# Delta-rule heads of a two-layer diffusion backbone: the two head pairs computed in step instead of one after the other

## The chip, the cores and the metric

One core of a Trainium2 chip runs the whole program in one launch. The metric is the device time of that core in microseconds (us), median of several executions.

## The reference, cut to what matters

Two layers over 256 context and 256 latent tokens. Each layer projects the normed tokens (`w_in`), feeds three groups of heads (A: softmax attention, B: HGRN2 recurrence, C: gated DeltaNet), projects their outputs (`w_out`), and ends with a gated MLP with a short convolution. The change is in group C: four heads of width 64, both directions, chunks of 64 tokens. For one head and one chunk, in short form:

```
kk    = einsum('bhtd,bhsd->bhts', k, k)
tri   = eye(c) + where(strict, beta * kk * decay, 0)
sol   = triangular_solve(tri, [v * beta, k * beta * exp(gc)])     # u, w
v_new = u - w @ state
out   = (q * exp(gc)) @ state + ((q k^T) * decay) @ v_new
state = exp(g_last) * state + (k * exp(g_last - gc))^T @ v_new
```

## The kernel before, in words

Activations lie transposed, 128 channels on the partitions and 512 tokens along a row, columns 0 to 255 context and 256 to 511 latent. A dense product (`dense`, `dense_gen`, L276 to L296) takes a weight block split into a rounded high part and a rest (`wload`: a DMA on SP's queue, a cast on ScalarE, a subtraction on VectorE or GpSimd) and issues three matmuls for each 128 channels, L292 to L294 in the projections of the heads.

Group C has four heads in two pairs. A pair lies on the 128 partitions, one head on partitions 0 to 63 (its lower half), the other on 64 to 127. `gdn` (L594 to L754) works on one pair and is run for pair 0, then for pair 1 (`gd` in `mixers`, L1132). Inside, it runs over the context half and the latent half of the tokens, four chunks each, both directions at once:

- a prologue (L621 to L650): decay matrices `E1`, `X`; the cumulative decay `gb` by a matmul with the block matrix `bones`; token-major copies of k and v (`relay`); the product `kk`;
- the inverse of `tri` by doubling (L663 to L690). Five levels each have a product `rt`, a masking on VectorE (L679), a product `dT`, and a subtraction on VectorE (L689) into `MT`; beside them a copy on ScalarE (L684) and a transpose on VectorE (L685) feed `dT`;
- a scan over four chunks (L708 to L736): `ks` = k times state, two VectorE operations (L716), `vn` = the solved rows, a copy on ScalarE (L720), `kv` = k times the new values, two VectorE operations (L734) for the next state;
- the output products `go` (L749).

Each of these is a set of 64x64 matmuls. A matmul whose operands lie on one half and whose result lies on one half uses one quarter of the 128x128 array, a corner. `bmm` (L518) issues them for both heads of the pair: rows 0 to 63 to columns 0 to 63, and rows 64 to 127 to columns 64 to 127, so two of the four corners. Both write one PSUM bank, each its own half. Group B's products (`hs` L847, `hu`, `ho`) use all four corners, its `hs` with one bank for each half of the rows. The trace counts two matmul instructions for each such fp32 matmul, so a row of the order with x8 is x16 in the trace.

What sets the order: `weave` (L1025) takes steps from several generators in turn, in the shares of the table `RATE` (in-projections, group C, group B, attention, modulation; the sixth number is group C's share while only projections run beside it); the framework's scheduler then fixes each engine's order. TensorE executes its matmuls in that order, so one that has to wait holds up all behind it. Group C's pages have the tag `g` (5 pages, 4 taken by a pair and half); 512-column temporaries share `r2` (16).

Of the kernel before, what the change touches and what calls it, by code (L numbers as in the profile page):

```python
# [20 lines left out]
P = 128  # L21
# [13 lines left out]
R2, RAW, WHI, WLO = 16, 4, 3, 2  # L35
# [9 lines left out]
RATE = ((103, 220, 32, 136, 15, 12), (69, 192, 60, 63, 5, 9))  # L45
# [35 lines left out]
for _name, _w in (("ident", 128), ("ones", 128), ("sel", 2), ("sel8", 16), ("eps", 1), ("one", 1), ("bones", 128),  # L81
                  ("perm", 128), ("i64", 64), ("inc2", 128), ("ninc2", 128), ("pstr2", 128), 
# [7 lines left out]
def constants():  # L90
# [10 lines left out]
    put("bones", same)  # L101
    pm = np.zeros((P, P))
# [41 lines left out]
class Kernel:  # L144
    def __init__(self, ctx, tc, I, out, dbg=None):
# [6 lines left out]
        self.BUFS = {"h": 8, "g": 5, "fk": 2, "qk": 5, "kq": 2, "r2": R2, "d2": 3, "g2": 3, "h2": 5, "hv": 2, "vt": 2, "hq": 1, "ht": 1, "raw": RAW, "whi": WHI, "wlo": WLO}  # L152
        self.uid = 0
        self.ring = itertools.cycle(["g"] * 5 + ["kq"] * 2 + ["fk"] * 4)
# [369 lines left out]
    def relay(self, p, dst, srcs):  # L524
# [69 lines left out]
    def gdn(self, ly, hp, G, kq, v, last, res):  # L594
        nc = self.nc
        k, q = kq[:, 0, :], kq[:, 1, :]
        o = None
        ck = lambda t: t.rearrange("p (c t) -> p c t", t=64)
        hgm = self.C("hgm").rearrange("p (l t) -> p l t", t=64)
        for t, scale, l in ((k, 1.0, 0), (q, 0.125, NCTX if last else 0)):  # L600
            sq = self.tmp("g2", "l2")
            nc.scalar.activation(sq[:, l:], t[:, l:], AF.Square)
            ps = self.bank("g", "l2")
            nc.tensor.matmul(ps[:, l:], self.C("bones"), sq[:, l:], start=True, stop=True)
            self.act(sq[:, l:], ps[:, l:], AF.Ln, bias=self.C("eps"))
            self.act(sq[:, l:], sq[:, l:], AF.Exp, scale=-0.5)
            nc.vector.scalar_tensor_tensor(t[:, l:], t[:, l:], scale, sq[:, l:], ALU.mult, ALU.mult)
        yield
        carry = None
        for hf in range(2):  # L610
            out = hf == 1 or not last
            sel = lambda n: G[n][:, 16 * hp + 8 * hf:16 * hp + 8 * hf + 8]
            b64 = lambda n: sel(n).unsqueeze(2).to_broadcast([P, 8, 64])
# [3 lines left out]
            kc, qc, vc = (ck(t[:, 256 * hf:256 * hf + 256]) for t in (k, q, v))  # L617
            pA, pB = self.pg("g", "gA"), self.pg("g", "gB")
            E1, X = pA[:, 0:512], pA[:, 512:1024]
            eG, tok = pB[:, 0:512], pB[:, 512:1024]  # L620
            nc.vector.tensor_tensor(s4(E1), m4("inc2"), sel("la").rearrange("p (s c) -> p s c", s=2).unsqueeze(3).to_broadcast([P, 2, 4, 64]), ALU.mult)  # L621
            pb = self.bank("g", "gb")
            nc.tensor.matmul(pb, self.C("bones"), E1, start=True, stop=True)
            self.act(eG, pb, AF.Exp)
            nc.vector.tensor_tensor(ck(X), ck(pb), b64("gc"), ALU.subtract)
            yield
            self.relay("g", tok, [(k, 256 * hf, 256 * hf + 256), (v, 256 * hf, 256 * hf + 256)])
            ktok, vtok = ck(tok[:, 0:256]), ck(tok[:, 256:512])
            yield
            if out:  # L630
                for s in range(2):
                    nc.vector.scalar_tensor_tensor(s4(E1)[:, s], s4(X)[:, s], 0.0, m4("ninc2")[:, s], ALU.min, ALU.add)
                self.act(E1, E1, AF.Exp)
            for s in range(2):
                nc.vector.scalar_tensor_tensor(s4(X)[:, s], s4(X)[:, s], 0.0, m4("pstr2")[:, s], ALU.max, ALU.add)
            self.act(X, X, AF.Exp, scale=-1.0)
            nc.gpsimd.tensor_tensor(ck(X), ck(X), b64("beta"), ALU.mult)
            N = X[:, 0:256]
            nc.vector.tensor_tensor(N, X[:, 0:256], X[:, 256:512], ALU.add)
            pk = self.bank("g", "kk")  # L640
            n2 = 2 if out else 1
            pkv = pk.rearrange("p (c s t) -> p c s t", s=2, t=64)
            for c in range(4):
                a = 256 * hf + 64 * c
                for h in (0, 64):
                    nc.tensor.matmul(pkv[h:h + 64, c, 0:n2, :], k[h:h + 64, a:a + 64], kq[h:h + 64, 0:n2, a:a + 64], start=True, stop=True)
            nc.vector.tensor_tensor(ck(N), ck(N), pkv[:, :, 0, :], ALU.mult)
            if out:
                nc.vector.tensor_tensor(s4(E1), s4(E1), two(pkv[:, :, 1, :]), ALU.mult)
            yield  # L650
            gl = self.small("gl", 8, 4)
            ap = eG[:, 0:1]
# [4 lines left out]
            qe, SC = ck(eG), ck(E1)
            pC = self.pg("g", "gC")
            MT, Mx, mtx = pC[:, 0:512], pC[:, 512:768], pC[:, 768:1024]
            nc.scalar.copy(ck(MT), self.C("i64").unsqueeze(1).to_broadcast([P, 8, 64]))  # L660
            Nv, MTv = ck(N), ck(MT)
            for lev in range(LEVELS):
                b = 1 << lev  # L663

                def joint(c0, c1, bit0):
                    ap = MT[:, 256 * bit0 + 64 * c0:256 * bit0 + 64 * c0 + 1]
# [4 lines left out]
                rt = self.tmp("g2", "rt")[:, 0:256]  # L671
                if lev:
                    ps = self.bank("g", "rt")
                    self.bmm(ck(ps), lambda c: Nv[:, c, :], lambda c: joint(c, c + 1, 0), range(4))
                    src = ps[:, 0:256]
                else:
                    src = mtx
                    nc.vector.transpose(mtx, N)
                nc.vector.tensor_tensor(ck(rt), ck(src), hgm[:, lev, :].unsqueeze(1).to_broadcast([P, 4, 64]), ALU.mult)  # L679
                if lev == 0:  # L680
                    nc.vector.tensor_tensor(joint(0, 4, 0), joint(0, 4, 0), nb(rt), ALU.subtract)
# [5 lines left out]
                ps2 = self.bank("g", "dT")  # L687
                self.bmm(ck(ps2), lambda c: ck(Mx)[:, c, :], lambda c: ck(rt)[:, c, :], range(4))
                nc.vector.tensor_tensor(joint(0, 4, 0), joint(0, 4, 0), nb(ps2[:, 0:256]), ALU.subtract)  # L689
                yield  # L690
            pF = self.pg("g", "gF")
            kt, R, U, Sst = pF[:, 0:512], pF[:, 512:1024], X, pC[:, 512:1024]

            def scaled(dst, src, n):
                nc.gpsimd.tensor_tensor(s4(dst), two(src), sel(n).rearrange("p (s c) -> p s c", s=2).unsqueeze(3).to_broadcast([P, 2, 4, 64]), ALU.mult)

            scaled(R, vtok, "beta")
            scaled(kt, ktok, "kd")
            yield
            rv, uv, kv, sv = ck(R), ck(U), ck(kt), ck(Sst)  # L700
# [687 lines left out]
```

## Time and profile before

| | |
|---|---|
| time, median of 3 runs | 1443.58 us (1442.61 to 1451.51) |
| the profiled execution, its own time | 1446.47 us |
| its span, first to last instruction | 1444.7 us |
| TensorE matmuls busy | 1349.8 us, 93% |
| VectorE, ScalarE, GpSimd busy | 898.0, 650.4, 390.5 us |
| chain of work that ended last | PE 74%, DVE 14%, ACT 4%, POOL 3%, DMA 3%, issue 2% |

PE is TensorE, DVE VectorE, ACT ScalarE, POOL GpSimd. The span falls into stages: first projections of layer 0 up to 78 us, its three head groups with the rest of the projections from 78 to 400, the out-projection and MLP to 875, the first projections of layer 1 to 930, its head groups to 1190, the rest to the end. Group C runs in the two head stages alone.

### The profile page before, as it was taken

How to read it: one execution, taken by the hardware profiler on the slowest of the kernel's cores; microseconds unless marked ns; L12 is line 12 of the kernel's file. 1: busy time of each engine (PE TensorE's matmuls, PEld its weight loads, DVE VectorE, ACT ScalarE, POOL GpSimd, SP SyncE). 2: the span in 40 equal slices, each digit the busy share in tenths (PEclk: the TensorE clock that was granted, in tenths of full speed). 3: DMA queues.
4: the chain of work that ended last, by engine and by line, in shares of the span. 5: the costliest groups of instructions: out<-in, count | busy, mean ns of one | idle time of the engine just before them, and what ended most of it. 6: DMA issues, size and time to landing. Idle time of an engine off the chain costs nothing.

```text
span 1444.7 us, 26549 instructions
## 1 busy us (share of the span) xinstructions
PE 1349.8 (93%) x10712; PEld 1073.9 (74%) x10712; DVE 898.0 (62%) x1721; ACT 650.4 (45%) x1169; POOL 390.5 (27%) x370
## 2 busy tenths in 40 slices
PE   5999989999998999999999988999899989899996
PEld 2777656666787678888888887986676647799995
DVE  3573576858557775435544568766887635676765
ACT  4362424534365544324423446663353335565553
POOL 1020032201055222202210365111411005555554
PEclk8999999999899999999999999999999989999998
DMA  8512413222246663333323334532211255465552
GB/s 303 189 59 88 148 43 105 88 88 104 82 134 209 208 208 109 103 94 96 102 90 100 102 121 152 158 125 97 91 59 73 75 201 207 133 187 177 190 173 76
DMA packets 56283, 185.90 MB, mean 129 GB/s; under 512 B 6368, under 2 KB 10464, under 8 KB 56160
## 3 DMA queue, kind: packets, MB, share of 16 engines
q1 hardware_dynamic: 56160, 184.20, 38.6%
q8 instruction: 84, 1.38, 0.4%
q14 instruction: 39, 0.32, 0.1%
HBM read 182.08 MB, written 2.10 MB: 127 GB/s over the span
## 4 chain that ended last, share of the span: by engine, by line
PE 74%; DVE 14%; ACT 4%; POOL 3%; DMA 3%; issue 2%; SPq 0%; DVEq 0%; POOLq 0%; ACTq 0%
PE up L283 8%; PE up L284 8%; PE up L282 8%; PE in L292 6%; PE in L294 5%; PE in L293 5%; PE dn L284 4%; PE dn L283 4%; PE dn L282 4%; PE ada L316 2%; DVE wlo L272 2%; PE sc L993 2%; PE dT L522 1%; DMA raw<-ada_w 1%; PE rt L522 1%
## 5 line engine op out<-in xcount | busy, mean ns | idle before, releaser
L272 DVE TENSOR_TENSOR wlo<-raw,whi 128x1024 fp32r<-128x1024 f32 (+2 forms) x241 | 296.7, 1232 | 271.6 <-issue 93.8
L268 ACT CAST whi<-raw 128x1024 fp32r<-128x1024 f32 (+1 forms) x244 | 249.1, 1023 | 136.0 <-PE dn L284 98.9
L284 PE MATMUL up<-h,whi 128*128 128x256 f32 (+1 forms) x768 | 249.0, 325 | 1.3 <-DVE h L440 0.7
L282 PE MATMUL up<-h,whi 128*128 128x256 f32 (+1 forms) x768 | 248.5, 324 | 1.2 <-ACT h L437 1.1
L283 PE MATMUL up<-h,wlo 128*128 128x256 f32 (+1 forms) x768 | 248.1, 324 | 0.9 <-DVE wlo L272 0.9
L292 PE MATMUL in<-h,whi 128*128 128x512 f32 (+1 forms) x496 | 183.8, 371 | 2.5 <-DVE kq L476 2.2
L272 POOL TENSOR_TENSOR wlo<-raw,whi 128x256 fp32r<-128x256 f32 (+1 forms) x111 | 128.4, 1158 | 194.8 <-ACT whi L268 90.3
L293 PE MATMUL in<-h,wlo 128*128 128x512 f32 (+1 forms) x496 | 176.4, 356 | 1.1 <-DVE wlo L272 0.9
L294 PE MATMUL in<-h,whi 128*128 128x512 f32 (+1 forms) x496 | 177.3, 358 | 0.0
L282 PEld LDWEIGHTS up<-h,whi 128*128 128x128 f32 x768 | 145.9, 190 | 19.4 <-issue 4.2
L284 PEld LDWEIGHTS up<-h,whi 128*128 128x128 f32 x768 | 146.1, 190 | 16.5 <-issue 1.7
L283 PEld LDWEIGHTS up<-h,wlo 128*128 128x128 f32 x768 | 146.0, 190 | 15.7 <-issue 2.5
L283 PE MATMUL dn<-gT,wlo 128*128 128x256 f32 (+1 forms) x400 | 128.4, 322 | 3.4 <-DVE wlo L272 3.4
L282 PE MATMUL dn<-gT,whi 128*128 128x256 f32 (+1 forms) x400 | 128.5, 322 | 2.7 <-ACT gT L299 2.7
L284 PE MATMUL dn<-gT,whi 128*128 128x256 f32 (+1 forms) x400 | 128.2, 321 | 0.7 <-POOL gT L301 0.7
L1220 POOL TENSOR_TENSOR u<-u 128x512 f32<-128x512 f32 (+1 forms) x44 | 44.4, 1009 | 279.4 <-DVE u L476 257.9
L292 PEld LDWEIGHTS in<-h,whi 128*128 128x128 f32 x496 | 95.0, 191 | 21.7 <-issue 6.9
L294 PEld LDWEIGHTS in<-h,whi 128*128 128x128 f32 x496 | 95.1, 192 | 12.9 <-issue 1.5
L293 PEld LDWEIGHTS in<-h,wlo 128*128 128x128 f32 x496 | 95.3, 192 | 11.4 <-DVE wlo L272 1.9
L472 ACT ACTIVATE u<-up,vec 128x256 f32<-128x256 f32 (+1 forms) x96 | 61.8, 644 | 75.2 <-PE up L284 75.2
L283 PEld LDWEIGHTS dn<-gT,wlo 128*128 128x128 f32 x400 | 77.5, 194 | 9.2 <-DVE wlo L272 4.0
L282 PEld LDWEIGHTS dn<-gT,whi 128*128 128x128 f32 x400 | 77.5, 194 | 8.2 <-ACT gT L299 3.1
(278 smaller groups left out, 2414.2 us busy)
## 6 DMA issues: line engine op xcount, KB each, us to landing
raw<-ada_w SPq DMA_DIRECT2D x96, 512.0 KB, 4.3
raw<-w_up SPq DMA_DIRECT2D x96, 512.0 KB, 3.5
raw<-w_in SPq DMA_DIRECT2D x68, 512.0 KB, 3.7
raw<-w_down SPq DMA_DIRECT2D x32, 512.0 KB, 3.5
raw<-w_out SPq DMA_DIRECT2D x24, 512.0 KB, 3.6
raw<-w_down SPq DMA_DIRECT2D x24, 384.0 KB, 3.0
x<-xT SPq DMA_DIRECT2D x16, 256.0 KB, 5.8
x_spill<-x SPq DMA_DIRECT2D x8, 128.0 KB, 2.1
```

What stands on the lines that cost most here:

```text
L268: nc.scalar.copy(hi[:, :cols], raw[:, :cols])
L272: e.tensor_sub(lo[:, a:b], raw[:, a:b], hi[:, a:b].bitcast(F32))
L282: nc.tensor.matmul(ps, wh[:, k, :], ah, start=first and k == ks[0], stop=False)
L283: nc.tensor.matmul(ps, wl[:, k, :], ah, start=False, stop=False)
L284: nc.tensor.matmul(ps, wh[:, k, :], al, start=False, stop=last and k == ks[-1])
L292: nc.tensor.matmul(ps, wh[:, k, :], ah, start=k == 0, stop=False)
L293: nc.tensor.matmul(ps, wl[:, k, :], ah, start=False, stop=False)
L294: nc.tensor.matmul(ps, wh[:, k, :], al, start=False, stop=k == n - 1)
L316: nc.tensor.matmul(ps[32 * g:32 * g + 32, :], self.cs[:, k, :], w[:, kk, :], start=k < 4, stop=k >= 4, tile_position=(0, 32 * g))
L472: nc.scalar.activation(dst, ps, AF.Identity, scale=w3[1], bias=bias)
L522: self.nc.tensor.matmul(pv[h:h + 64, n], l[h:h + 64], r[h:h + 64], start=True, stop=True)
L1220: self.nc.gpsimd.tensor_mul(us[0][:, lo:], us[0][:, lo:], us[1][:, lo:])
```

## The change

`gdn` takes both pairs and does every step for pair 0 and pair 1 together. Pair 1's heads are exchanged: gates, `alog`, `dt` and the token-major copies of its pair stand on the other half, so that its products go from rows 0 to 63 to columns 64 to 127 and from rows 64 to 127 to columns 0 to 63. A new `quad` issues the matmuls of a chunk for both pairs, each pair with a bank of its own. `vn` keeps the same half for rows and columns in both pairs; the part of `go` that reads pair 1's state has become a product `gi` of its own, added by VectorE. New are a matrix `obones` and a matmul `gs` (exp(gc) of pair 1 on exchanged halves), and two half-height copies on ScalarE instead of one full copy for pair 1 at each level.

Pages: `g` 7 instead of 5 (seven taken by a half), `r2` 14 instead of 16, group B's page `ht` gone (its folds go into the page of `F2`), the output of group C is written over q, four of the eight `y` tiles of out-projection and MLP lie in the page `hq`. `RATE` is set anew.

```diff
-R2, RAW, WHI, WLO = 16, 4, 3, 2
+R2, RAW, WHI, WLO = 14, 4, 3, 2
-RATE = ((103, 220, 32, 136, 15, 12), (69, 192, 60, 63, 5, 9))
+RATE = ((121, 197, 32, 218, 37, 8), (53, 64, 15, 50, 5, 7))
-                    ab.append(kind + d * 4 + hp * 2 + h2)
+                    ab.append(kind + d * 4 + hp * 2 + (h2 ^ hp))
-        self.BUFS = {"h": 8, "g": 5, "fk": 2, "qk": 5, "kq": 2, "r2": R2, "d2": 3, "g2": 3, "h2": 5, "hv": 2, "vt": 2, "hq": 1, "ht": 1, "raw": RAW, "whi": WHI, "wlo": WLO}
+        self.BUFS = {"h": 8, "g": 7, "fk": 2, "qk": 5, "kq": 2, "r2": R2, "d2": 3, "g2": 3, "h2": 5, "hv": 2, "vt": 2, "hq": 1, "raw": RAW, "whi": WHI, "wlo": WLO}
+    def new_ys(self):
+        t = self.pg2("hq", "y")
+        return [t[:, 512 * i:512 * i + 512] for i in range(4)] + [self.tmp("r2", "y") for i in range(4)]
+    def quad(self, items):
+        for out, l, r, start, stop in items:
+            self.nc.tensor.matmul(out, l, r, start=start, stop=stop)
-    def gdn(self, ly, hp, G, kq, v, last, res):
+    def gdn(self, ly, G, kq, v, last, res):
+        HP = range(2)
+        H = [slice(0, 64), slice(64, 128)]
...
+                nc.vector.tensor_tensor(ck(X[hp]), ck(pb), b64(hp, "gc"), ALU.subtract)
+                if hp:
+                    pb = self.bank("g", "gs")
+                    nc.tensor.matmul(pb, bones[1], E1[hp], start=True, stop=True)
+                self.act(eG[hp], pb, AF.Exp)
...
-                    ps = self.bank("g", "rt")
-                    self.bmm(ck(ps), lambda c: Nv[:, c, :], lambda c: joint(c, c + 1, 0), range(4))
+                    ps = [self.bank("g", "rt") for hp in HP]
+                    for c in range(4):
+                        self.quad((ck(ps[hp])[H[g ^ hp], c, :], Nv[hp][H[g], c, :], joint(MT[hp][H[g]], c, c + 1, 0), True, True)
+                                  for hp in HP for g in range(2))
...
-                nc.scalar.copy(nb(mtx), joint(0, 4, 1))
-                nc.vector.transpose(Mx, mtx)
+                nc.scalar.copy(nb(mtx[0]), joint(MT[0], 0, 4, 1))
+                for g in range(2):
+                    nc.scalar.copy(nb(mtx[1][H[1 - g]]), joint(MT[1][H[g]], 0, 4, 1))
+                for hp in HP:
+                    nc.vector.transpose(Mx[hp], mtx[hp])
...
+                ps = [self.bank("g", "vn") for hp in HP]
+                for hp in HP:
+                    for s, j in enumerate(js):
+                        self.quad((ck(ps[hp])[H[g], s, :], MTv[hp][H[g], j, :], rv[hp][H[g], j, :], True, True) for g in range(2))
+                    nc.scalar.copy(pair(U[hp], i), ck(ps[hp][:, 0:128]))
...
         def gd():
+            go = {}
+            yield from self.gdn(ly, G, kq, gv, last, go)
             for hp in range(2):
-                go = {}
-                yield from self.gdn(ly, hp, G, kq[hp], gv[hp], last, go)
                 mix[6 + hp] = self.head_end(go[hp], self.V(ly, "gdn"), gg[hp], 1.0 / 64, self.C("bones"), qlo, "g", "r2", "g")
```

How the rows of an engine stand now, at three places. First TensorE in the context half of layer 0, at the first `rt` with a matmul (`in` is a dense product, `gC` holds `MT`, `gA` holds the matrix to invert). Before, pair 0 alone:

```order
L293 MATMUL in_891<-h_131,wlo_888 128x512
L294 MATMUL in_891<-h_131,whi_887 128x512
L522 MATMUL rt_902<-gC_871,gA_741 64x64 x8
L292 MATMUL in_891<-h_132,whi_887 128x512
L293 MATMUL in_891<-h_132,wlo_888 128x512
```

The same place of the changed kernel:

```order
L294 MATMUL in_1081<-h_136,wlo_1078 128x512
L295 MATMUL in_1081<-h_136,whi_1077 128x512
L602 MATMUL rt_1109<-gC_1053,gA_814 64x64 x2
L602 MATMUL rt_1110<-gC_1054,gA_815 64x64 x2
L602 MATMUL rt_1109<-gC_1053,gA_814 64x64 x2
L602 MATMUL rt_1110<-gC_1054,gA_815 64x64 x2
L602 MATMUL rt_1109<-gC_1053,gA_814 64x64 x2
L602 MATMUL rt_1110<-gC_1054,gA_815 64x64 x2
L602 MATMUL rt_1109<-gC_1053,gA_814 64x64 x2
L602 MATMUL rt_1110<-gC_1054,gA_815 64x64 x2
L293 MATMUL in_1141<-h_129,whi_1137 128x512
```

The eight matmuls of pair 1, which stood some hundred rows further down, now alternate with pair 0's two by two, so that four neighbours take four corners. In 28 of the 40 sets of `rt` and `dT` they stand so throughout, in 8 the first few stand pair by pair, in 4 all of one pair stand before the other's.

Second, TensorE in the scan, the same half (`kq` holds k and q, `gF` the right-hand sides). Before, one chunk of pair 0:

```order
L522 MATMUL ks_1344<-gC_871,kq_140 64x64 x4
L292 MATMUL in_1385<-h_129,whi_1381 128x512
L293 MATMUL in_1385<-h_129,wlo_1382 128x512
L294 MATMUL in_1385<-h_129,whi_1381 128x512
L522 MATMUL vn_1351<-gF_1276,gC_871 64x64 x4
L292 MATMUL in_1385<-h_130,whi_1381 128x512
L293 MATMUL in_1385<-h_130,wlo_1382 128x512
L522 MATMUL kv_1364<-gA_741,gF_1276 64x64 x4
```

Of the changed kernel, `vn` and `kv` of a chunk, with a modulation product between:

```order
L602 MATMUL vn_1545<-gF_1521,gC_1053 64x64 x4
L602 MATMUL vn_1546<-gF_1521,gC_1054 64x64 x4
L317 MATMUL ada_1557<-raw_1558,cs 32x512 x2
L317 MATMUL ada_1557<-raw_1562,cs 32x512 x2
L317 MATMUL ada_1557<-raw_1566,cs 32x512 x2
L317 MATMUL ada_1557<-raw_1570,cs 32x512 x2
L602 MATMUL kv_1584<-gA_814,gB_816 64x64 x2
L602 MATMUL kv_1585<-gA_815,gB_817 64x64 x2
L602 MATMUL kv_1584<-gA_814,gB_816 64x64 x2
L602 MATMUL kv_1585<-gA_815,gB_817 64x64 x2
```

`kv` alternates between the pairs, `vn` does not; each set now holds both pairs and has one stretch of other work behind it instead of two.

Third, VectorE between two levels (`wlo` is the split of a weight block). Before:

```order
L689 TENSOR_TENSOR gC_871<-gC_871,dT_947 128x64x2x2
L685 STREAM_TRANSPOSE gC_871<-gC_871 128x256
L272 TENSOR_TENSOR wlo_1033<-raw_1030,whi_1032 128x1024
L679 TENSOR_TENSOR rt_973<-rt_974,consts 128x256
```

Of the changed kernel, a later level:

```order
L721 TENSOR_TENSOR gC_1053<-gC_1053,dT_1293 128x32x2x4
L721 TENSOR_TENSOR gC_1054<-gC_1054,dT_1294 128x32x2x4
L494 COPY raw_1193<-in_1200 128x512
L714 STREAM_TRANSPOSE gC_1053<-gC_1053 128x256
L704 TENSOR_TENSOR rt_1313<-rt_1315,consts 128x256
L704 TENSOR_TENSOR rt_1314<-rt_1316,consts 128x256
L714 STREAM_TRANSPOSE gC_1054<-gC_1054 128x256
```

The VectorE operations of a level are as many as before, but both pairs' stand in one row of work: the next product waits for two of each instead of one.

## Rows read from the trace of the kernel before

**Rows 1.** The two head stages by engine; columns as in its header row.

```profile
core 0: us, PE busy (x) PEld busy (x) DVE busy (x) ACT busy (x) POOL busy (x), PEclk, DMA share, GB/s
78.00:400.00 322.00, 303.89 (x3084) 214.66 (x3084) 209.09 (x508) 134.60 (x291) 49.76 (x42) 0.96 0.26 90
930.00:1190.00 260.00, 247.29 (x2619) 173.05 (x2617) 175.08 (x447) 109.30 (x229) 40.83 (x37) 0.97 0.30 103
```

**Rows 2.** Group C's 64x64 products by line: count, busy us, mean ns, idle before.

```profile
L522 PE MATMUL rt<-gC,gA 64*64 64x64 f32 x640 | 27.8, 226 | 11.9 <-DVE gC L681 8.5 <-DVE ssm L1001 2.2 <-DVE gC L689 0.9
L522 PE MATMUL vn<-gF,gC 64*64 64x64 f32 x256 | 18.8, 242 | 1.3 <-DVE gF L716 1.3
L522 PE MATMUL ks<-gC,kq 64*64 64x64 f32 x224 | 14.1, 238 | 0.3 <-DVE gC L707 0.2
L646 PE MATMUL kk<-kq 64*64 64x128 f32 x96 | 6.5, 275 | 0.0
L749 PE MATMUL go<-gA 64*64 64x64 f32 x192 | 11.6, 221 | 0.0
L749 PE MATMUL go<-gB,gC 64*64 64x64 f32 x176 | 10.7, 218 | 0.0
```

**Rows 3.** Timeline of PE, a set of 16 in dense work: start, us, what.

```profile
114.37 0.39 PE L294 MATMUL in<-h,whi 128*128 128x512 f32 x1
114.69 0.68 PE L522 MATMUL dT<-rt,gC 64*64 64x64 f32 x16
115.30 0.50 PE L292 MATMUL in<-h,whi 128*128 128x512 f32 x1
115.64 0.39 PE L293 MATMUL in<-h,wlo 128*128 128x512 f32 x1
```

**Rows 4.** Timeline of PE, a set of 8.

```profile
159.28 0.40 PE L293 MATMUL in<-h,wlo 128*128 128x512 f32 x1
159.51 0.40 PE L294 MATMUL in<-h,whi 128*128 128x512 f32 x1
159.84 0.45 PE L522 MATMUL ks<-gC,kq 64*64 64x64 f32 x8
160.21 0.50 PE L292 MATMUL in<-h,whi 128*128 128x512 f32 x1
160.55 0.39 PE L293 MATMUL in<-h,wlo 128*128 128x512 f32 x1
```

**Rows 5.** Timeline of PE, group B's 64 in four corners.

```profile
184.68 0.40 PE L294 MATMUL in<-h,whi 128*128 128x512 f32 x1
185.01 1.16 PE L847 MATMUL hs<-raw,kd 64*64 64x64 f32 x64
186.10 0.50 PE L292 MATMUL in<-h,whi 128*128 128x512 f32 x1
186.43 0.39 PE L293 MATMUL in<-h,wlo 128*128 128x512 f32 x1
```

**Rows 6.** Timeline of PE, full-array fp32 products of 128 columns.

```profile
1158.23 1.95 PE L1018 MATMUL do<-wt,vt 128*128 128x128 f32 x16
1160.01 0.60 PE L967 MATMUL vt<-consts,raw 128*128 128x128 f32 x4
```

**Rows 7.** Group C's VectorE operations between products, by line.

```profile
L689 DVE TENSOR_TENSOR gC<-gC,dT 128x256 f32<-128x256 f32 x40 | 16.7, 417 | 23.5 <-PE dT L522 23.5
L685 DVE STREAM_TRANSPOSE gC<-gC 128x256 f32<-128x256 f32 x40 | 17.5, 438 | 8.7 <-ACT gC L684 8.5
L716 DVE SCALAR_TENSOR_TENSOR gF<-ks,sbe,gF 128x64 f32<-128x64 f32 x56 | 13.9, 278 | 14.7 <-PE ks L522 14.5
```

**Rows 8.** Timeline of PE, the first product after a prologue.

```profile
194.10 1.12 PE L522 MATMUL rt<-gC,gA 64*64 64x64 f32 x16 [4.97 <-DVE gC L681]
```

**Rows 9.** Two stretches with the clock at its lower level for a part.

```profile
188.00:201.00 13.00, 8.03 (x81) 5.75 (x80) 8.16 (x14) 2.67 (x5) 4.65 (x3) 0.74 0.12 40
375.00:400.00 25.00, 24.77 (x312) 17.82 (x313) 13.43 (x48) 11.57 (x37) 0.73 (x1) 0.73 0.29 100
```

More of the change, by code (lines that the diff above doesn't have):

```diff
@@ L101, in constants @@
     put("bones", same)
+    put("obones", ~same)
     pm = np.zeros((P, P))
@@ L608, in gdn @@
-        yield
-        carry = None
+        H = [slice(0, 64), slice(64, 128)]
+        for ts, scale, l in ((k, 1.0, 0), (q, 0.125, NCTX if last else 0)):
+            for t in ts:
+                sq = self.tmp("g2", "l2")
+                nc.scalar.activation(sq[:, l:], t[:, l:], AF.Square)
+                ps = self.bank("g", "l2")
+                nc.tensor.matmul(ps[:, l:], self.C("bones"), sq[:, l:], start=True, stop=True)
+                self.act(sq[:, l:], ps[:, l:], AF.Ln, bias=self.C("eps"))
+                self.act(sq[:, l:], sq[:, l:], AF.Exp, scale=-0.5)
+                nc.vector.scalar_tensor_tensor(t[:, l:], t[:, l:], scale, sq[:, l:], ALU.mult, ALU.mult)
+            yield
@@ L634, in gdn @@
[L634 to L640, printed above, removed]
+            kc, qc, vc = ([ck(t[:, 256 * hf:256 * hf + 256]) for t in ts] for ts in (k, q, v))
@@ new lines, in gdn @@
+            yield
+            for hp in HP:
+                self.relay("g", tok[hp], [(t[hp], 256 * hf, 256 * hf + 256) for t in (k, v)], hp)
+                yield
+            ktok, vtok = [ck(t[:, 0:256]) for t in tok], [ck(t[:, 256:512]) for t in tok]
+            for hp in HP:
+                if out:
+                    for s in range(2):
+                        nc.vector.scalar_tensor_tensor(s4(E1[hp])[:, s], s4(X[hp])[:, s], 0.0, m4("ninc2")[:, s], ALU.min, ALU.add)
+                    self.act(E1[hp], E1[hp], AF.Exp)
+                for s in range(2):
+                    nc.vector.scalar_tensor_tensor(s4(X[hp])[:, s], s4(X[hp])[:, s], 0.0, m4("pstr2")[:, s], ALU.max, ALU.add)
+                self.act(X[hp], X[hp], AF.Exp, scale=-1.0)
+                nc.gpsimd.tensor_tensor(ck(X[hp]), ck(X[hp]), b64(hp, "beta"), ALU.mult)
@@ L641, in gdn @@
+            N = [t[:, 0:256] for t in X]
+            pk = [self.bank("g", "kk") for hp in HP]
             n2 = 2 if out else 1
-            pkv = pk.rearrange("p (c s t) -> p c s t", s=2, t=64)
+            pkv = [t.rearrange("p (c s t) -> p c s t", s=2, t=64) for t in pk]
             for c in range(4):
                 a = 256 * hf + 64 * c
-                for h in (0, 64):
-                    nc.tensor.matmul(pkv[h:h + 64, c, 0:n2, :], k[h:h + 64, a:a + 64], kq[h:h + 64, 0:n2, a:a + 64], start=True, stop=True)
@@ L657, in gdn @@
[L657 to L661, printed above, removed]
+                self.quad((pkv[hp][H[h ^ hp], c, 0:n2, :], k[hp][H[h], a:a + 64], kq[hp][H[h], 0:n2, a:a + 64], True, True)
+                          for hp in HP for h in range(2))
+            for hp in HP:
+                nc.vector.tensor_tensor(N[hp], X[hp][:, 0:256], X[hp][:, 256:512], ALU.add)
+                nc.vector.tensor_tensor(ck(N[hp]), ck(N[hp]), pkv[hp][:, :, 0, :], ALU.mult)
+                if out:
+                    nc.vector.tensor_tensor(s4(E1[hp]), s4(E1[hp]), two(pkv[hp][:, :, 1, :]), ALU.mult)
@@ new lines, in gdn @@
+            yield
+            gl = [self.small("gl", 8, 4) for hp in HP]
+            pC = [self.pg("g", "gC") for hp in HP]
+            MT, Mx, mtx = ([t[:, a:b] for t in pC] for a, b in ((0, 512), (512, 768), (768, 1024)))
+            for hp in HP:
+                ap = eG[hp][:, 0:1]
+                nc.gpsimd.tensor_copy(gl[hp].rearrange("p (s c) -> p s c", s=2),
+                                      bass.AP(tensor=ap.tensor, offset=ap.offset, ap=[list(ap.ap[0]), [256 + 63, 2], [64, 4]]))
+                nc.scalar.copy(ck(MT[hp]), self.C("i64").unsqueeze(1).to_broadcast([P, 8, 64]))
@@ new lines, in gdn @@
+                for hp in HP:
+                    nc.vector.transpose(Mx[hp], mtx[hp])
+                yield
+                ps2 = [self.bank("g", "dT") for hp in HP]
+                for c in range(4):
+                    self.quad((ck(ps2[hp])[H[g ^ hp], c, :], ck(Mx[hp])[H[g], c, :], ck(rt[hp])[H[g], c, :], True, True)
+                              for hp in HP for g in range(2))
+                for hp in HP:
+                    nc.vector.tensor_tensor(joint(MT[hp], 0, 4, 0), joint(MT[hp], 0, 4, 0), nb(ps2[hp][:, 0:256]), ALU.subtract)
@@ L690, in gdn @@
                 yield
             pF = self.pg("g", "gF")
[L692 to L698, printed above, removed]
+            R, U, Sst = [pF[:, 512 * hp:512 * hp + 512] for hp in HP], X, [t[:, 512:1024] for t in pC]
@@ L706, in gdn @@
             if carry is not None:
-                nc.vector.tensor_copy(pair(Sst, 0), ck(carry))
+                for hp in HP:
+                    nc.vector.tensor_copy(pair(Sst[hp], 0), ck(carry[hp]))
             for i in range(4):
@@ L1256, in ffn @@
             if ys is None:
-                ys = self.ys = [self.tmp("r2", "yf") for m in range(KT)]
+                ys = self.ys = self.new_ys()
             def down(ss, a, b):
@@ L1310, in run @@
             hT = self.new_pages()
-            self.ys = [self.tmp("r2", "y") for m in range(KT)]
+            self.ys = self.new_ys()
             pending = self.sub_layer(ly, 0, lo, lambda ss, a, b: self.out_proj(ly, mix, ss, a, b), hT)
```

177 lines of the change are left out of this document (84 added, 93 removed).

## The prediction, made before the changed kernel was run

> **What bounds the kernel now.** I read the busy shares by stage first, then the timeline of TensorE (PE) inside the head stages, then what its small products cost there. In the two stages in which group C runs, 322 and 260 us long, PE is busy 303.89 and 247.29 us, so it is idle 18 and 13 us; VectorE (DVE) is busy 209.09 and 175.08 us, about two thirds [rows 1]. PE executes in a fixed order. These stages are therefore as long as the work of PE in them, plus about 31 us in which it waits, plus what a lower clock adds. A cheaper small product moves everything behind it forward, as long as its operands are not late.
>
> **What a set of small products costs.** The dense work around them has a pitch of 0.23 us (159.28 to 159.51) [rows 4]. A set of 16 in two corners moves the second dense matmul behind it from where it would be by 115.64 - 114.37 - 2 x 0.23 = 0.81 us [rows 3]. A set of 8 costs 160.55 - 159.51 - 0.46 = 0.58 us [rows 4]. So eight more cost 0.23 us, 0.029 each, and what is left, 0.81 - 16 x 0.029 = 0.35 us, is paid once for each set: PE runs empty before it and after it. Group B's set of 64 in four corners costs 186.43 - 184.68 - 0.46 = 1.29 us [rows 5]; less 0.35 that is 0.0147 each, half of the pace in two corners. Four corners do run together in this kernel, and the pace of 0.029 is the array's and not that of issuing.
>
> **The change, part by part.**
>
> *The inverse.* `rt` and `dT` (its count is the same) are 640 instructions each, 80 sets of 16 [rows 2]: 80 x 0.81 = 65 us, of which I take off 3 us for sets that stand right beside another small product and share the 0.35. After, 40 sets of 32. By the order 28 alternate throughout, 0.35 + 32 x 0.0147 = 0.82 us; 8 begin pair by pair, I take 1.0; 4 have all of one pair first and cost two sets of 16, 1.62. Together 23 + 8 + 6.5 = 37.5 us. Saved: 24 us.
>
> *The scan.* `ks` and `kv` (same count) are 56 sets of 8 [rows 2], 56 x 0.58 = 32.5 us. After, 28 sets of 16 in four corners at 0.35 + 16 x 0.0147 = 0.585 us, but 8 of them are cut by other work and count as two sets of 8: 20 x 0.585 + 8 x 1.16 = 21 us. Saved: 11.5 us. `vn` is 32 sets of 8 [rows 2], a third of them cut in two by a dense matmul (0.35 more): 18.6 + 3.8 = 22.4 us. After, it stays in two corners and only the sets join: 12 x 0.81 + 4 x 1.16 = 14.4 us. Saved: 8 us.
>
> *Prologue and output.* `kk` has six sets of 16 with 128 columns (0.35 + 16 x 0.058 = 1.28 us) and two with 64 (0.81), 9.3 us [rows 2]; after 3 x 1.28 + 2 x 0.81 = 5.5. Saved: 3.8 us. `go` is 192 + 176 instructions in six sets [rows 2], 368 x 0.029 + 6 x 0.35 = 12.8 us; after, the 192 take four corners (2.8), the 176 stay in two (5.1), with seven switches (2.5): 10.4. Saved: 2.4 us. New is `gs`, four fp32 matmuls of 512 columns. 16 full-array instructions of 128 columns take 1160.01 - 1158.23 = 1.78 us, 0.111 each [rows 6]; 512 columns are 0.445, two instructions 0.89, four times 3.6 us. Added: 3.6 us.
>
> Sum for PE: 24 + 11.5 + 8 + 3.8 + 2.4 - 3.6 = **46 us less**.
>
> *VectorE, ScalarE, GpSimd.* Their operations are as many as before, apart from 20 copies on ScalarE, the adding of `gi` and GpSimd's scaling in two parts. What changes is the wait of one product for the next. Between `rt` and `dT` stand a masking (the same form as L689's 0.417 us) and a transpose (0.438); with both pairs two of each, 0.85 us more. Between `dT` and `rt` a second subtraction, 0.42; around the scan two more operations of 0.278 on either side, 0.56 [rows 7]; from `vn` to `kv` a second copy on ScalarE, taken as 0.28, the size of these. With 20, 20, 14, 14 and 16 such steps that is 17 + 8.4 + 7.8 + 7.8 + 4.5 = 45 us more latency in joined steps. The cover is dense work: by the order most joined sets have 3 to 11 matmuls of 0.23 us, or a modulation or attention product, behind them, and there are half as many sets to cover. I cost it at nothing; with the cover gone it would be those 45 us.
>
> *Prologues.* The worst wait of PE is here: 4.97 us before the first product of pair 0's latent half, on DVE [rows 8]; all of `rt` waits 11.9 us, 8.5 of it there [rows 2]. There were eight prologues, now four with twice the DVE work. Each layer's first is covered by 60 to 90 dense matmuls, the latent ones only by about what one pair had. I take no change, with bounds of 8 us less (these waits gone) and 10 us more (two of 5 us grow to 10).
>
> *Pages, folds, `y` tiles.* At nothing: gates and `y` are read in the MLP, behind whole sets of dense matmuls; the reload of x for the residual is issued behind six of `w_out`'s blocks as before. If the seven pages of `g` make a latent prologue wait for the context half's last reader, its first two DVE operations are late by under 2 us twice.
>
> **A rule that speaks against it.** The pairs of two-corner products write the upper and lower half of one bank. A row of 128 columns takes 0.111 us on the full array [rows 6], so 64 columns take 0.056; these sets run at 0.029, two at a time [rows 3, 4], although both row halves write one bank. The Trainium skill, "TensorEngine Tiling (Array Packing)", section "Gotcha 1: PSUM Pressure", says that different row tiles cannot access the same PSUM bank at once. By that rule the new quads, whose two row halves share each pair's bank, would not overlap as group B's do (its `hs` has a bank for each half). The trace speaks against the rule; it is the first rival.
>
> **The rivals.**
>
> *1. Four corners in this bank layout run no faster than two.* For it: only group B shows four, and with its banks laid out otherwise. Against: the two-corner sets already overlap in one bank [rows 3, 4]. Then only joined sets save: the inverse 61.7 - (36 x 1.28 + 6.5) = 9, `ks` and `kv` 32.5 - 25.5 = 7, `vn` 8, `kk` 1, less 3.6: 21.5 us. About 1422.
>
> *2. The freed time is half lost to waits.* DVE's 209 us would be 70% of a stage of 297 and its operations come in rows for both pairs; half of the 45 us uncovered gives 1398 + 23 = 1421. Against: the order places other work in nearly every step. The Trainium skill warns of this in the same page, section "PSUM Bottleneck": tiling speeds up TensorE but not the reading of PSUM.
>
> *3. More is won.* The clock was granted at 0.74 over 13 us just after the 4.97 us wait and at 0.73 over 25 us of almost only small products [rows 9]. The lower of the two levels, 1.2 GHz, is half of 2.4: it held for 0.26/0.5 x 13 = 6.8 and 0.27/0.5 x 25 = 13.5 us and cost half of that, 10 us. With that gone and one 5 us wait too, 1383.
>
> *4. Slower: the joined latency decides.* All 84 steps uncovered cost 45 us, two latent prologues late by 10 more each cost 20: 65 against 46, 1446 + 19, about 1462. It decides once the waits grow by more than 61 us (46 and 1%), 0.7 us a step. Against: PE is idle only 31 us in both stages, the waits of all five products together a fraction of that.
>
> **How the numbers follow.** The profiled execution took 1446.5 us (span 1444.7), 2.9 above the median of the runs shown. 1446.5 - 46 = 1400.5; against the median 1443.6 - 46 = **1398 us**. Chances: forecast 0.58 (1385 to 1412 by the bounds of the prologues and some us of steps), rival 1 0.12, rival 2 0.14, rival 3 0.10, rival 4 0.06. The range for 8 in 10 runs from rival 3 to a little beyond rivals 1 and 2: 1380 to 1428. Measurement tells about 1% here, 14 us; faster than 1429 holds all of the forecast and rival 3 and most of rivals 1 and 2: 0.86; within 1%: 0.08; slower: 0.06.
>
> **What would show it.** A set of 32 `rt` in dense work should cost 0.8 us and 64-column fp32 in quads 0.015 us each; 0.029 proves rival 1. The head stages should shrink from 322 and 260 us to about 298 and 238 with PE idle still near 30 us; PE idle of 50 us or more, charged to DVE before `rt`, `dT` or `ks`, proves rival 2 or 4. The other stages should stay within 5 us. I am wrong if the stages shrink by a different cause, such as the clock, or if the MLP moves.

## The result and the profile after

The changed kernel took 1394.67 us (median of four runs, 1389.14 to 1397.04) against 1443.17 us: a ratio of 0.9645, 95% interval 0.9599 to 0.9692, or 51 us less (44 to 58). The ratio weighs all executions, one of 1451.51 us among them; the medians alone differ by 48.5 us. The profiled execution took 1397.04 us, its span is 1395.3 us; before 1446.47 and 1444.7. So the trace has a difference of 49.4 us to explain.

The stages first, between the same points of the program, which lie elsewhere in time: from 75 us to layer 0's last `op` (out-projection) product, and layer 1 from its first `gb` to 26 us ahead of its last `op`. The kernel before (columns: stretch, us, busy of PE, PEld, DVE, ACT, POOL, granted clock, DMA share, GB/s):

```profile
75.00:466.20 391.20, 368.52 (x3556) 270.38 (x3555) 250.71 (x575) 177.26 (x380) 90.09 (x80) 0.97 0.31 105
941.00:1189.70 248.70, 235.99 (x2508) 163.04 (x2507) 166.74 (x415) 100.82 (x214) 40.83 (x37) 0.97 0.30 101
```

The changed kernel:

```profile
75.00:453.30 378.30, 350.70 (x3565) 258.75 (x3563) 248.13 (x576) 182.14 (x391) 92.23 (x84) 0.96 0.32 109
925.80:1139.40 213.60, 199.90 (x2472) 146.44 (x2472) 161.97 (x408) 101.12 (x210) 45.57 (x41) 0.98 0.34 116
```

Layer 0 gave 12.9 us, layer 1 35.1. PE's idle time in them (length less busy) went from 22.7 + 12.7 = 35.4 to 27.6 + 13.7 = 41.3 us: the waits grew by 6 us, while PE's work shrank by 54.

The products of group C, by line (they answer [rows 2]):

```profile
L602 PE MATMUL rt<-gC,gA 64*64 64x64 f32 x640 | 18.6, 236 | 9.4 <-DVE gC L707 8.3 <-DVE gC L721 0.9
L602 PE MATMUL vn<-gF,gC 64*64 64x64 f32 x256 | 12.2, 225 | 0.4 <-DVE gF L748 0.3
L602 PE MATMUL ks<-gC,kq 64*64 64x64 f32 x224 | 8.4, 237 | 0.0
L602 PE MATMUL kk<-kq 64*64 64x128 f32 x96 | 4.3, 273 | 0.4 <-ACT gB L544 0.4
L602 PE MATMUL go<-gA 64*64 64x64 f32 x192 | 5.7, 225 | 0.0
L643 PE MATMUL gs<-gA,consts 128*128 128x512 f32 x8 | 4.4, 632 | 0.1
```

One instruction still takes its 220 to 240 ns; `rt` as a whole is busy 18.6 instead of 27.8 us, since four run beside one another. A set of both pairs in dense work, on PE's timeline (the answer to [rows 3]):

```profile
167.13 0.39 PE L295 MATMUL in<-h,whi 128*128 128x512 f32 x1
167.45 0.69 PE L602 MATMUL rt<-gC,gA 64*64 64x64 f32 x32
168.08 0.50 PE L293 MATMUL in<-h,whi 128*128 128x512 f32 x1
168.42 0.39 PE L294 MATMUL in<-h,wlo 128*128 128x512 f32 x1
```

168.42 - 167.13 - 0.46 = 0.83 us for 32, as much as 16 cost before.

What came instead is the wait ahead of layer 0's latent `rt`, 8.32 us for the 4.97 of [rows 8], and the clock behind it, 0.57 over 16 us for the 0.74 over 13 of [rows 9]:

```profile
233.47 0.87 PE L602 MATMUL rt<-gC,gA 64*64 64x64 f32 x10 [8.32 <-DVE gC L707]
```

```profile
229.00:245.00 16.00, 11.53 (x135) 8.13 (x136) 11.38 (x39) 9.58 (x21) 0.92 (x1) 0.57 0.12 38
```

### The profile page after: what moved, and what is told of

The parts are those of the page before. It is cut to its first block, busy times and chain, and to the rows that moved or that the text cites. A ratio compares the mean times of both kernels' runs of the same rounds, so it can differ in the third digit from the quotient of the medians.

```text
span 1395.3 us, 26653 instructions
## 1 busy us (share of the span) xinstructions
PE 1298.6 (93%) x10720; PEld 1048.0 (75%) x10720; DVE 892.5 (64%) x1722; ACT 658.9 (47%) x1189; POOL 393.7 (28%) x378
## 4 chain that ended last, share of the span: by engine, by line
PE 74%; DVE 12%; ACT 5%; POOL 4%; issue 2%; DMA 2%; SPq 0%; DVEq 0%; POOLq 0%; ACTq 0%
PE up L284 8%; PE up L283 8%; PE up L285 8%; PE in L293 6%; PE in L294 5%; PE in L295 5%; PE dn L285 4%; PE dn L284 4%; PE dn L283 4%; PE ada L317 2%; DVE wlo L273 2%; PE sc L1035 2%; PE op L284 1%; PE op L283 1%; PE op L285 1%
## 5 line engine op out<-in xcount | busy, mean ns | idle before, releaser
L273 DVE TENSOR_TENSOR wlo<-raw,whi 128x1024 fp32r<-128x1024 f32 (+2 forms) x241 | 299.8, 1245 | 269.1 <-issue 90.4
L294 PEld LDWEIGHTS in<-h,wlo 128*128 128x128 f32 x496 | 96.2, 194 | 12.7 <-issue 3.5
```

What stands on the lines that cost most here:

```text
L273: e.tensor_sub(lo[:, a:b], raw[:, a:b], hi[:, a:b].bitcast(F32))
L294: nc.tensor.matmul(ps, wl[:, k, :], ah, start=False, stop=False)
```

## The experiments

Every ratio is to the kernel before on the same chip, with its 95% interval; the changed kernel has 0.9645. 0.001 is 1.44 us.

### Four corners against two

Pair 1's heads are not exchanged; the order of TensorE differs from the changed kernel's in three places only.

```diff
-  self.quad((ck(ps[hp])[H[g ^ hp], c, :], Nv[hp][H[g], c, :], ...
+  self.quad((ck(ps[hp])[H[g], c, :], Nv[hp][H[g], c, :], ...      # likewise kk, dT, ks, kv, go, the gates
```

> The changed kernel with pair 1's heads not exchanged: the same instructions in nearly the same order on TensorE, but all 64x64 products go to two corners of the array. Theory A (four neighbours in four corners run at half the price of two): the 28 whole sets of 32 rt and dT cost 0.35 + 32 x 0.029 = 1.28 instead of 0.83 us, the 20 whole sets of ks and kv 0.81 instead of 0.585, go's 192 instructions 5.6 instead of 2.8, kk 1 to 3 more: together 13 + 2 + 4.5 + 2.8 + 2 = 24 us more than the changed kernel's 1395, about 1419. Rival (four corners no faster than two, the gain is all from joined sets, order and rates): 1395, within 5. Rival (waits decide): longer products hide in waits, under 10 more.

Measured: 1410.82 us, 0.9773 (0.9745 to 0.9801). Its timeline of PE at the set shown above:

```profile
156.69 0.39 PE L293 MATMUL in<-h,whi 128*128 128x512 f32 x1
157.01 1.15 PE L602 MATMUL rt<-gC,gA 64*64 64x64 f32 x32
158.09 0.50 PE L294 MATMUL in<-h,wlo 128*128 128x512 f32 x1
158.43 0.40 PE L295 MATMUL in<-h,whi 128*128 128x512 f32 x1
```

158.43 - 156.69 - 0.46 = 1.28 us, to the hundredth what the price of two corners gives. The four corners are worth 0.0128, 18 us for the forecast 24, which lies within the two intervals; PE is idle 33.3 us in the two stages instead of 41.3, so part of the shorter products went into waits. The rival "four corners no faster than two" falls. This kernel, which has the joined sets and all else, is 33 us faster than before.

### All of one pair, then all of the other

```diff
-  for c in range(4):
-      self.quad(... for hp in HP for g in range(2))
+  for hp, c in itertools.product(HP, range(4)):
+      self.quad(... for g in range(2))
```

> The changed kernel, heads exchanged, with kk, rt, dT, ks and kv issued all of pair 0 first and then all of pair 1; go as it was. Theory A (four corners help only while neighbours in TensorE's order lie in different corners): these sets cost what they do in the run with heads not exchanged, 16 to 22 us more than the changed kernel's 1395 without go's 3: 1408 to 1414. Rival (products of the second pair start in their own corners as soon as they are free, far ahead in the order): 1395 to 1400.

Measured: 1402.58 us, 0.9679 (0.9654 to 0.9705), about 5 us slower than the changed kernel; the expectation was three times that, and the intervals overlap. The timeline of PE says why, first an `rt`:

```profile
157.41 0.40 PE L294 MATMUL in<-h,wlo 128*128 128x512 f32 x1
157.74 0.98 PE L602 MATMUL rt<-gC,gA 64*64 64x64 f32 x32
158.64 0.50 PE L295 MATMUL in<-h,whi 128*128 128x512 f32 x1
158.98 0.40 PE L293 MATMUL in<-h,whi 128*128 128x512 f32 x1
```

Then a `kv`:

```profile
184.89 0.39 PE L295 MATMUL in<-h,whi 128*128 128x512 f32 x1
185.21 0.47 PE L602 MATMUL kv<-gA,gB 64*64 64x64 f32 x16
185.62 0.50 PE L293 MATMUL in<-h,whi 128*128 128x512 f32 x1
185.95 0.40 PE L294 MATMUL in<-h,wlo 128*128 128x512 f32 x1
```

And a `kv` of the changed kernel, in alternating order:

```profile
191.08 0.40 PE L295 MATMUL in<-h,whi 128*128 128x512 f32 x1
191.41 0.46 PE L602 MATMUL kv<-gA,gB 64*64 64x64 f32 x16
191.80 0.50 PE L293 MATMUL in<-h,whi 128*128 128x512 f32 x1
192.13 0.40 PE L294 MATMUL in<-h,wlo 128*128 128x512 f32 x1
```

`rt` costs 158.98 - 157.41 - 0.46 = 1.11 us, between 0.83 and 1.28; `kv` costs 185.95 - 184.89 - 0.46 = 0.60, no more than the 192.13 - 191.08 - 0.46 = 0.59 of the alternating order. Late operands do not make the difference: in 19 of the 20 whole sets of `ks` and `kv` in this trace the second pair's first product starts 0.03 us after the first pair's, in 24 of the 29 of `rt` and `dT` 0.29 to 0.31 us after, with ten of the first pair's sixteen begun. Eight instructions of the one pair ahead of the other's keep nothing back, sixteen do in part. The exact alternation is worth a third of what I thought, by the ratios, which overlap; the exchange of the halves does the rest.

### The layout alone

The kernel before with the pages, the folds, group C's output over q and the `y` tiles of the changed one, `gdn` and `RATE` as before.

```diff
-R2, RAW, WHI, WLO = 16, 4, 3, 2
+R2, RAW, WHI, WLO = 14, 4, 3, 2
...
-        T1 = self.pg2("ht", "T1", w=1056)
...
-                o = self.tmp("r2", "go")
+                o = q
...
-                ys = self.ys = [self.tmp("r2", "yf") for m in range(KT)]
+                ys = self.ys = self.new_ys()
```

> The kernel before with only the layout edits: 7 pages g, 14 r2, group B's folds in the page of F2, group C's output over q, four y tiles in the page hq; gdn pair after pair and the old rates. Forecast of the prediction: nothing, 1443 within 3. Rival: the 5 us that the first MLP lost and the 4 of the out-projection come from these pages: 1434 to 1439.

Measured: 1455.68 us, 1.0080 (1.0054 to 1.0107): 11.5 us slower, where both expected nothing or a gain. Its windows of layer 1's head stage and of a part of it:

```profile
945.40:1203.80 258.40, 245.35 (x2508) 169.56 (x2508) 166.52 (x414) 100.47 (x214) 39.77 (x37) 0.93 0.30 98
1036.00:1060.00 24.00, 22.50 (x210) 15.64 (x210) 13.99 (x46) 5.66 (x11) 4.97 (x5) 0.57 0.30 97
```

Over these 24 us the clock was granted at 0.57, so 20.6 us at 1.2 GHz, which cost half of that, 10 us; the kernel before has 1.00 at the same place, and its stage is 9.7 us shorter:

```profile
1032.00:1056.00 24.00, 23.05 (x292) 16.34 (x284) 16.82 (x54) 9.40 (x21) 4.35 (x3) 1.00 0.41 140
```

Right ahead of that stretch, the timeline of PE of this run shows a wait that the kernel before hasn't at this place:

```profile
1037.13 0.27 PE L527 MATMUL ks<-gC,kq 64*64 64x64 f32 x2 [2.43 <-DVE gC L713]
```

Then PE ran mostly 64x64 products with one or two dense ones between. In this profile the layout's cost in this stage is the clock. That need not hold for every execution: one of the four took 1452.97 us at a mean granted clock of 0.976, no lower than in the profile of the kernel before.

One of its edits alone, the folds:

```diff
-              half(T1[:, 1024:1056])]
+              half(Fp[:, 1920:1984]), half(self.small("Tw", 32, 1))]
...
-            if lev:
-                fold(lev + 1)
+            fold(lev + 1)
             yield
```

> The kernel before with one layout edit alone: group B's folds go into the page of F2, each at the end of its level, and the page ht is gone. Theory A (the 11 us that all layout edits together cost come from an order that is a little different in layer 1, where TensorE then ran 20 us at the lower clock): the folds are the one layout edit that changes work inside the head stage, so 1450 to 1458 with a long stretch at the lower clock near 1040 us. Rival (the pages and y tiles cost it): 1442 to 1447, no such stretch.

Measured: 1446.16 us, 1.0017 (0.9986 to 1.0047). But its ten executions fall into two groups: six took 1444.4 to 1446.8 us at a mean granted clock of 0.975 to 0.978, four took 1453.4 to 1458.7 us at 0.967 to 0.969, as low as the layout's lowest. The profile is of one of the six and has no such stretch of the clock. So the folds cost nothing in those six. Whether the four had the layout's stretch, no trace shows; that the folds bring it at times is not ruled out, and what the pages and tiles add is open.

### The rates

```diff
-RATE = ((121, 197, 32, 218, 37, 8), (53, 64, 15, 50, 5, 7))
+RATE = ((103, 220, 32, 136, 15, 12), (69, 192, 60, 63, 5, 9))     # in the changed kernel
```

> The changed kernel with the RATE table of the kernel before. Theory A (the gain lies in the price of the sets): 1395 to 1405, the sets stay whole and only waits move. Rival B (the order set by the new rates brought a good part, above all the 32 us of layer 1's head stage where 22 were forecast and 12 us of modulation products that no longer run at the lower clock): 1410 to 1425.

Measured: 1417.45 us, 0.9812 (0.9788 to 0.9836). So 27 of the 51 us are there with the old table, and the new one brings 24. Its windows of the two stages:

```profile
75.00:454.20 379.20, 351.15 (x3566) 255.59 (x3565) 253.06 (x577) 184.02 (x392) 91.78 (x84) 0.98 0.34 108
930.10:1160.50 230.40, 212.13 (x2497) 152.01 (x2496) 159.28 (x412) 101.53 (x216) 40.62 (x41) 0.99 0.32 106
```

Layer 0 is as long as with the new table (378.3), layer 1 is 16.8 us longer: 12.2 of PE's work and 4.6 of waits. Rival B was right on the time and on layer 1, but not on the clock: with the old table it was granted at 0.99 in layer 1's stage, with the new one at 0.98. The other way round, the new table in the kernel before:

> The kernel before with the RATE table of the changed kernel. Theory A: 1443 within 8, since the products cost what they did. Rival B (rates bring a good part by themselves): 1415 to 1430.

Measured: 1483.25 us, 1.0265 (1.0232 to 1.0297), 38 us slower; neither expectation. The table fits the steps of both pairs and is worth nothing by itself: PE idles 67.6 us in the two stages there, for 35.4 before, and the clock in layer 1 is granted at 0.91. Why layer 1 gains, one guess: the old table leaves three modulation blocks to the end of its heads.

```diff
-RATE = ((103, 220, 32, 136, 15, 12), (69, 192, 60, 63, 5, 9))
+RATE = ((103, 220, 32, 136, 15, 12), (69, 192, 60, 63, 15, 9))    # in the run with the old table
```

> The changed kernel with the RATE table of the kernel before, but the share of the modulation in layer 1 raised from 5 to 15. Theory A (of the 23 us that the old table costs, about 8 are the three modulation blocks that run one behind another at the end of layer 1's heads, waiting for their weights): they move among the other work, 1417 falls to 1407 to 1411. Rival B (the old table costs through the sets of group C, which lie in the first 135 us of that stage): 1414 to 1420.

Measured: 1416.60 us, 0.9819 (0.9795 to 0.9842), no gain. The blocks did move forward, but attention was left alone at the end, and PE waited for its softmax on VectorE:

```profile
1151.87 1.87 PE L1035 MATMUL sc<-qk 64*128 64x512 f32 x4
1156.90 1.09 PE L1052 MATMUL wt<-consts,em 128*128 128x128 f32 x4 [3.15 <-DVE em L1048]
```

Which of the old shares costs the 17 us is open, but the traces of the changed kernel with either table show where PE's 12 us of work go. With the old table layer 1's `rt` and `dT` stand on TensorE in 38 unbroken stretches, with the new one in 22, group B's `hs` in 32 and 16: sets are cut, and each piece pays the fixed price again. From start to next start, waits left out, from the first `gb` to the last `op`, `rt`, `dT`, `ks`, `kv`, `vn` and `hs` take 5.6 us more, the modulation (`ada`) 5.5 us more.

### The wait of 8 us in layer 0

In the changed kernel, GpSimd ahead of that wait (its timeline):

```profile
214.56 1.05 POOL L658 TENSOR_TENSOR gA<-gA,sbeta 128x512 f32<-128x512 f32 x1 [2.13 <-ACT gA L222]
215.56 3.70 POOL L727 TENSOR_TENSOR gF<-gB,sbeta 128x512 f32<-128x512 f32 x1
219.34 2.63 POOL L729 TENSOR_TENSOR gB<-gB,skd 128x256 f32<-128x256 f32 x1
221.93 2.02 POOL L727 TENSOR_TENSOR gF<-gB,sbeta 128x512 f32<-128x512 f32 x1
223.92 1.87 POOL L729 TENSOR_TENSOR gB<-gB,skd 128x256 f32<-128x256 f32 x3
225.75 1.04 POOL L658 TENSOR_TENSOR gA<-gA,sbeta 128x512 f32<-128x512 f32 x1
```

L658 of pair 1 belongs to the prologue, the L727 and L729 ahead of it to the scan, which begins after the last `rt`, at 271 us. So I put L658 of pair 1 on VectorE:

```diff
-  nc.gpsimd.tensor_tensor(ck(X[hp]), ck(X[hp]), b64(hp, "beta"), ALU.mult)
+  (nc.vector if hp else nc.gpsimd).tensor_tensor(ck(X[hp]), ck(X[hp]), b64(hp, "beta"), ALU.mult)
```

> The changed kernel with one multiplication by beta per half (pair 1's, in the prologue) on VectorE instead of GpSimd. Theory A (the 8.32 us wait before the latent half's first rt in layer 0 comes from GpSimd's queue: pair 1's multiplication stands behind five scalings that the scan alone needs, 215.6 to 225.8 us): the wait falls below 2 us and the 13.7 us at the lower clock right behind it shorten, 8 to 15 us less than the changed kernel's 1395, so 1380 to 1387. Rival B (the latent prologue of two pairs is simply too long for its cover): the wait stays above 6 us, 1393 to 1397.

Measured: 1396.69 us, 0.9678 (0.9653 to 0.9704): no gain, and the wait is still there, charged to another row of VectorE:

```profile
231.30 1.42 PE L602 MATMUL rt<-gC,gA 64*64 64x64 f32 x24 [8.02 <-DVE ssm L1046]
```

Followed back through that trace, it is a chain across groups. Group B's scaling of K stands behind the same scalings on GpSimd (224.71 to 227.82):

```profile
224.71 3.11 POOL L930 TENSOR_TENSOR K<-K,F 128x512 f32<-128x512 f32 x2
```

ScalarE's queue waits for it with a copy, and the softmax activation stands behind that copy:

```profile
227.85 0.62 ACT L911 COPY kj<-K 128x512 f32<-128x512 f32 x1 [11.69 <-POOL K L930]
228.50 0.47 ACT L222 ACTIVATE em<-sc,smx 128x256 f32<-128x256 f32 x1
```

VectorE waits with the softmax's reciprocal, and pair 1's transpose stands behind it:

```profile
229.09 0.16 DVE L1043 RECIPROCAL ssm<-ssm 128x1 f32<-128x1 f32 x1 [4.07 <-ACT em L222]
229.17 0.13 DVE L1039 TENSOR_SCALAR smx<-smx 128x1 f32<-128x1 f32 x1
229.22 0.43 DVE L702 STREAM_TRANSPOSE gC<-gA 128x256 f32<-128x256 f32 x1
```

Taking one of two chains away changed nothing. Next the scalings themselves are made later, by reading beta and kd from a copy that needs the inverse's first level:

```diff
+  lat = [self.small("lat", 16) for hp in HP]                     # after level 0
...
+  nc.vector.scalar_tensor_tensor(lat[hp][:, a:a + 8], MT[hp][:, 0:1].to_broadcast([P, 8]), 0.0, sel(hp, n), ALU.mult, ALU.add)
...
-  nc.gpsimd.tensor_tensor(s4(R[hp]), two(vtok[hp]), bsc(hp, "beta"), ALU.mult)
+  nc.gpsimd.tensor_tensor(s4(R[hp]), two(vtok[hp]), lsc(hp, 0), ALU.mult)      # likewise kd
```

> The changed kernel with GpSimd's six scalings of a half (R and the scaled k) made to depend on the inverse's first level: they read beta and kd from a copy of 16 columns that VectorE makes after that level. Theory A (the wait of 8 us in layer 0's latent prologue stays in the run with beta on VectorE because two chains stand behind these scalings in GpSimd's queue: pair 1's multiplication by beta, and group B's scaling of K, on which ScalarE's kj copy, then a softmax activation, then VectorE's second transpose wait in their queues): the wait falls below 2.5 us, the lower clock behind it shortens, 6 to 14 us less than the changed kernel's 1395: 1381 to 1389. Rival B (the prologue is too long for its cover whatever stands on GpSimd): the wait stays at 6 to 8 us, 1392 to 1400.

Measured: 1389.57 us, 0.9614 (0.9589 to 0.9640), and half of the wait is gone:

```profile
229.83 0.87 PE L602 MATMUL rt<-gC,gA 64*64 64x64 f32 x10 [4.75 <-DVE gC L707]
```

The wait falls by 3.57 us, to about the 4.97 that the kernel before had; in the traces of the other runs on the changed kernel's new table, whose scalings stay early, it is 6.66 to 8.02 us. The stretch from 75 us to the last `op` of layer 0 falls from 378.3 to 373.9, but it is 374.2 in the run without `gs` too (below), where the wait is 7.78 us; so the stretch does not show what the wait is worth. Both theories have a half: GpSimd's queue made 3.6 us; in what is left VectorE has no pause from 213.6 to 226.9 us, with group B's and the attention's rows between the prologue's. No run took those away, so that half is read, not shown. The ratio is the best of all runs, but its interval overlaps the changed kernel's.

### The price of `gs`

```diff
-  pb = self.bank("g", "gs")
-  nc.tensor.matmul(pb, bones[1], E1[hp], start=True, stop=True)
-  self.act(eG[hp], pb, AF.Exp)
+  for g in range(2):
+      self.act(eG[hp][H[1 - g]], pb[H[g]], AF.Exp)              # pair 1
```

> The changed kernel without the matmul gs: exp(gc) of pair 1 is written to the exchanged halves by two half-height activations on ScalarE. Theory A (TensorE's work is the length of the stage): the four gs, 2.5 us from start to start in the trace of the changed kernel, go; 2 to 4 us less, 1391 to 1393. Rival B (the order that follows from any edit moves the clock by more than such a term): anything within 12 us of 1395, with the difference in the time at the lower clock.

Measured: 1390.45 us, 0.9626 (0.9603 to 0.9649), 2.7 us less by the ratios for the 3.6 of the forecast, but within the intervals. With the other edits of the last section:

> Both edits together: no gs and pair 1's multiplication by beta on VectorE. Theory A: the two gains add up, 1377 to 1385. Rival B: they do not, since the order moves: 1385 to 1400.

Measured: 1392.47 us, 0.9645 (0.9619 to 0.9672).

> Late scalings and no gs matmul (exp(gc) of pair 1 by two half-height activations). Theory A: both gains, from 1390 down to 1376 to 1384. Rival B: the wait stays, 1388 to 1394.

Measured: 1393.29 us, 0.9633 (0.9609 to 0.9657), though its wait is 4.6 us too. The small gains do not add up: the granted clock of these three profiles is 0.981, 0.976 and 0.974; 0.005 of 1390 us is 7 us of TensorE's full rate, more than each edit is worth.

## Why the prediction was right, and where it was not

The time lies 3 us from the forecast, partly by luck: errors of 11.5, 7 and 24 us largely cancel (point 3). The parts that stand behind it:

1. **The price of a set was right.** Expected and measured, in us: 32 `rt` or `dT` in four corners 0.82 and 0.82 to 0.84; begun pair by pair 1.0 and 1.06; 16 `ks` or `kv` 0.585 and 0.59; 16 `vn` 0.81 and 0.81; 32 `kk` 1.28 and 1.23; 32 in two corners 1.28 and 1.28. So two sets of 16 (1.62) lose 0.34 us by being joined and another 0.46 by the corners. In whole kernels the corners are worth 18 us, by the run with two.

2. **The bank rule did not hold here.** Both row halves write each pair's bank, its upper and its lower half, and the sets of 32 run at the four-corner price, 0.82 to 0.84 us. The Trainium skill, "TensorEngine Tiling (Array Packing)", section "Gotcha 1: PSUM Pressure", has different row tiles unable to use one PSUM bank at once; the trace of after disagrees with the rule as that of before did.

3. **The sum of 46 was right by compensation.** Along one path of runs: the layout alone costs 11.5 us (1.0080), the new `gdn` on that layout with the old rates brings 1.0080 - 0.9812 = 0.0268, 39 us, and the new rates 0.9812 - 0.9645 = 0.0167, 24 us. The step "costed at nothing" for the pages, folds and `y` tiles failed by 11.5, the sum for `gdn` by 7, and the rates had no term at all. PE's waits in the two stages grow by 9 us from the layout's profile to that with the old rates (37.2 to 46.3), so the waits, costed at nothing too, would account for the 7. By the sign that I had set, stages that shrink by a different cause, I was wrong for the rates' part. Steps of another path would have other sizes, as the new table in the old kernel shows.

4. **The stages came out the other way round.** I expected 24 us from layer 0 and 22 from layer 1; they gave 12.9 (9 of it ahead of most of the out-projection, 324 to 315 us) and 35.1. Layer 0 lost part of its gain to the 8.32 us wait and to the clock behind it. That is the bound I had named for the prologues, two waits of 5 growing to 10, in one place instead of two. Its growth came from GpSimd's queue, which I had not looked at for the prologues: with the scalings made late it is 4.75 us; what causes the rest is not shown. Layer 1 has the rates' 16.8 us on top; without them it gave 18.3, near the 22.

5. **The waits stayed covered.** PE's idle time grew by 6 of the possible 45 + 10 us; rivals 2 and 4 fall. Of rival 3 nothing came: the clock's stretches moved to other places, and the mean granted clock is 0.974 for 0.976.

6. **"The other stages within 5 us"** nearly held: the first MLP took 403.0 instead of 408.6 us from its first `up` to its last `dn`, with the clock at 1.00 instead of 0.99, the second 203.1 for 202.7.

7. **A slip in rival 4.** Its 1462 is the median 1443.6 + 19; 1446 + 19, as it stands there, is 1465. Nothing hangs on it.

## What to carry to other kernels

Price small products by the set: each had a fixed 0.35 us here, so joining two sets and giving the second the idle corners, by exchanging its data, took 1.62 us to 0.82; a strict alternation is not needed while the runs are short. After such a change set the order anew and look at each in-order queue, above all at early, unneeded work on a slow engine: it can stall TensorE through two other engines.

## What the hardware showed

- Products for other corners start before all of those ahead of them in the order have begun. With eight instructions of one pair ahead nothing is lost, 0.60 us for 16 pair by pair and 0.59 in alternation; with sixteen ahead it is 1.11 against 0.83.
- The clock can cost as much as an edit: 20.6 us at the lower level (0.57 over 24 us) came with a new page layout whose instructions on TensorE were as many (2508 in the stage), behind a wait of 2.43 us and in a stretch of mostly 64x64 products in which PE was busy 22.5 of 24 us. One program's executions can differ by as much: the folds alone took 1445 us at a granted clock of 0.977 or 1458 at 0.967.
- An operation of one form on GpSimd took from 1.05 to 3.70 us in the same prologue (L658 at 214.56, L727 at 215.56, both 128x512). The long ones lie where VectorE had no pause (211.2 to 223.6 us), but so does the short one at 214.56, beside VectorE's copies out of PSUM (L546); what sets the length is not shown.
